# Expert weights of a two-layer backbone: units of 512 KB beside transfers of two neighbouring units

## The chip, the core and the metric

The kernel runs on one core of one Trainium2 chip. Its engines are named as in the profile: PE (matrix), DVE (vector), ACT (scalar), POOL (gpsimd) and SP, whose queue issues the loads from the chip's memory (HBM) that this text is about. The metric is the device time of one execution in microseconds (us), as the median of several runs. All data is fp32.

## The reference, cut to what matters

Two layers over 256 latent tokens and 256 context tokens of width 1024. Layer 0 is a neighbourhood attention and a dense SwiGLU, layer 1 a recurrent block and a top-2-of-8 expert SwiGLU. The change touches the weights of the experts:

```python
def moe_ffn(h, w_router, b_router, w1, w3, w2):
    logits = (h @ w_router).astype(jnp.float32) + b_router.astype(jnp.float32)
    top_v, top_i = lax.top_k(logits, TOP_K)          # TOP_K = 2
    gates = jax.nn.softmax(top_v, axis=-1)
    ...
    for e in range(N_EXPERTS):                       # 8 experts
        y = y + comb[..., e:e + 1] * swiglu(h, w1[e], w3[e], w2[e])
    return y
# swiglu(h, w1, w3, w2) = (silu(h @ w1) * (h @ w3)) @ w2
# w1, w3: 1024 x 3584 and w2: 3584 x 1024 for each expert
```

So the experts' weights are 8 x 3 x 1024 x 3584 x 4 bytes = 352 MB, and all of them are read once.

## The kernel before

**Units.** Every weight is cut on the host into units of 128 partitions x 1024 values (4 KB in each partition, 512 KB in all). Of an expert's weights, a step `s` (seven of them, 512 hidden columns each) has four units of w1, four of w3 and four of w2, so an expert has 84 and all experts 672. The four w2 units of the very last step are laid out differently and come from a tensor of their own, `w2l` (keys "w2c"). In `moe`, the tensor of the other 668, each unit is one contiguous piece of 512 KB.

**Stream.** The class `Stream`, a kind of `Raws`, holds the list of all weight units in the order in which they are used, that of layer 0 and of the recurrent block first. `Raws.load` walks the list: for the next unit it takes the first pool with a free place, allocates a tile called `raw` there and issues the load on SP's queue (L247). A unit is released when it has been used, and its place goes to the next unit in the list. SP works in order: a load that waits for its place holds up all later loads. Each load also waits for one of eight semaphores in turn (DMAHW0 to DMAHW7 in the program's order), so at most eight loads are in flight.

**Places.** The places come from several pools: three of its own (`raw`), and memory that earlier stages leave: eight from the hidden state of the recurrent block (`hp`), four (`rawm`), two (`raw3`), six from the products of the recurrent block (`zp`, three opened first, then a fourth, then all), and for a short time five in tiles that the experts' inputs take later. That makes 23 in the experts' stage.

**Heavy and light experts.** Experts run in a fixed pattern of eight turns. In turns 0, 2, 4 and 6 (heavy; up to 128 tokens) each unit is split by ACT (`whi`, L303) and DVE (`wlo`, L314) into two parts, and PE makes three matmuls of each piece (L1825 to L1827 for w1 and w3, L1758 to L1760 for w2); the unit is released when DVE has made `wlo`. In turns 1, 3, 5 and 7 (light, `LIGHT`; up to 64 tokens) PE reads the raw unit itself (`pair`, L1738), and the unit is released when PE is done. `small_up` does a light step: four rounds of one unit of w1 and one of w3, the units standing in the list in the same order; `w2_step` takes the four w2 units of the step before, and `hidden` turns the step's result. `step` drops in small pieces of the expert before or after (`combine`, `gather`).

```python
            self.nc.sync.dma_start(t, ap() if callable(ap) else ap)      # L247, one unit
                parts.sort(key=lambda x: x[2])                           # light: w1 0, w3 0, w1 1, w3 1, ...
```

Of the kernel before, what the change touches and what calls it, by code (L numbers as in the profile page):

```python
# [117 lines left out]
def lay_out(i):  # L118
# [86 lines left out]
class Rows:  # L205
# [3 lines left out]
    def __getitem__(self, i):  # L209
        _, k, *s = i  # L210
        return self.tiles[k // 2][(slice(None), k % 2, *s)]


class Raws:
    def __init__(self, nc):
        self.nc = nc
        self.pools, self.units, self.raws = [], [], {}
        self.dma_at = self.at = 0

    def add_pool(self, pool, bufs, once=False, n=100, tag="raw", open=None):  # L220
        self.pools.append([pool, bufs if open is None else open, 0, once, bufs, tag])
        self.load(n)
        return self.pools[-1]

    def add_tiles(self, aps, again):
        self.pools.append([None, len(aps), 0, again, aps])
        self.load()

    def widen(self, r, n):
        r[1] = n  # L230
        self.load()

    def add(self, key, ap):
        self.units.append((key, ap))
# [118 lines left out]
def body(tc, nc, es, a, out, upto, dbg):  # L353
# [37 lines left out]
    hh = Rows([hp.tile([P, 2, 512], F32R, name="hh", tag="raw", bufs=8) for _ in range(4)])  # L391
    hl = Rows([hp.tile([P, 2, 512], F32R, name="hl", tag="raw", bufs=8) for _ in range(4)])
# [330 lines left out]
    def moe(p, *i):  # L723
        if p == 0:
            return a["moe"][(0, *i)]
        return lambda: a["moe"][(expert(p), *i)]
# [7 lines left out]
    def add_moe(key, ap):  # L734
        if key[1] in LIGHT:
            st.plain.add(key)
        st.add(key, ap)

    for p in range(NE):
        for s in range(NST):  # L740
            parts = [(nm_, z, i) for nm_, z in (("w1", 0), ("w3", 4)) for i in range(4)]
            if p in LIGHT:
                parts.sort(key=lambda x: x[2])
            for nm_, z, i in parts:
                add_moe((nm_, p, s, i), moe(p, s, z + i))
            if p or s:
                pe, q = divmod(p * NST + s - 1, NST)
                for i in range(4):
                    add_moe(("w2", pe, q, i), moe(pe, q, 8 + i))
    for c in range(4):  # L750
        add_moe(("w2c", NE - 1, c), lambda c=c: a["w2l"][expert(NE - 1), c])
# [17 lines left out]
    sm.add_pool(rawm, RM)  # L769
# [537 lines left out]

    def x_tile(t):
# [11 lines left out]
        xs_ = rawm.tile([P, 2, 512], F32R, name="xcs", tag="raw")  # L1320
        xh, xl_ = xs_[:, 0], xs_[:, 1]
# [38 lines left out]
    def post(q, ri):  # L1360
# [27 lines left out]
        def gated(o):  # L1388
            i, x = divmod(3 * q + o, 2)
            if x == 0:  # L1390
                zq[i] = zp.tile([P, 2, 2, NL], F32R, name="z", tag="raw", bufs=6)
            z = z_t[3 * q + o] = zq[i][:, x, 0], zq[i][:, x, 1]
            cut(*z, hf[o])
# [49 lines left out]
    for i, (kind, n) in enumerate(MIX):  # L1443
# [3 lines left out]
        elif kind == "x":  # L1447
# [6 lines left out]
            if n == 11:  # L1454
                st.add_pool(hp, 8)
            run(4, 3)
        elif kind == "a":
            run(100, 3)
            post(n, gates(n))
            if n == 3:  # L1460
                st.add_pool(rawm, RM)
# [3 lines left out]
                st.add_pool(raw3, RB3)  # L1465
        else:
            if n == (2, 0):
# [8 lines left out]
                once = mp.tile([P, 2, UNIT], F32, name="raw", tag="xs", bufs=1)  # L1476
                once = [once[:, i] for i in range(2)]
                once += [mp.tile([P, UNIT], F32, name="raw", tag=f"xe{y}", bufs=2) for y in "hl"]
                st.add_tiles(once, 4 * AG[0])
# [23 lines left out]
            if n == (0, 7):  # L1503
                zr = st.add_pool(zp, 6, open=3)
            if n == (1, 7):
                st.widen(zr, 4)
# [91 lines left out]
    def gather(p, k):  # L1598
        if k == 0:
            xe[p] = [mp.tile([P, KD, P], F32R, name=f"xe{y}", tag=f"xe{y}", bufs=2) for y in "hl"]  # L1600
# [47 lines left out]
    st.widen(zr, 6)  # L1648
# [162 lines left out]
    def step():  # L1811
        if side:
            side.pop(0)()
# [24 lines left out]
    def small_up(e, s):  # L1838
# [3 lines left out]
        for i in range(4):  # L1842
            for part, nm_ in ((0, "w1"), (1, "w3")):
                u = st.need((nm_, e, s, i))
                for kk in range(2):
                    k = 2 * i + kk
                    pair(
                        (acc[part][0:CAP], acc[part][CAP:P]), x[:, k, j],
                        [u[:, kk * 512 + h * NL:kk * 512 + h * NL + NL] for h in range(2)], k == 0, k == 7,
                    )  # L1850
                if i == 3 and part == 0:
                    sil = mp.tile([P, NL], F32, name="msil", tag="msil", bufs=1)
                    nc.scalar.activation(sil, acc[0], AF.Silu)
                if i == 3 and part == 1:
                    nc.vector.tensor_tensor(sil, sil, acc[1], ALU.mult)  # L1855
                st.done((nm_, e, s, i))
            step()
# [39 lines left out]
    def overflow(p):  # L1897
# [28 lines left out]

        def load(s, i):
            t = raw3.tile([P, UNIT], F32, name="raw", tag="raw")
            nc.sync.dma_start(t, a["moe"][expert(p) if p else 0, s, i])
            return t  # L1930
# [65 lines left out]
```

## Time and profile before

| what | us |
|---|---|
| median of 3 runs (1862.69 to 1865.57) | 1863.77 |
| the profiled execution | 1868.32 |
| its span, first to last instruction | 1866.4 |

| engine | busy us | share of the span | instructions |
|---|---|---|---|
| PE | 1779.2 | 95% | 10067 |
| DVE | 1187.4 | 64% | 1751 |
| ACT | 861.2 | 46% | 1263 |
| POOL | 188.0 | 10% | 195 |

The profiled execution took 4.55 us more than the median; 1.9 us of it lie outside its span. The loads on SP's queue moved 488.03 MB in 138464 packets. A busy PE can still be waiting: its matmuls are pipelined, and their ends are modelled. The experts' stage begins at about 908 us, with the first load of `moe`.

### The profile page before, as it was taken

To read this page: it belongs to the slowest core of one execution; us is meant where nothing else is said; L and a number is where in the kernel's file an instruction comes from. 1 tells how busy PE (TensorE), PEld (TensorE's weight loads), DVE (VectorE), ACT (ScalarE), POOL (GpSimd) and SP (SyncE) were. 2 spreads that over 40 slices of the span, in tenths; PEclk is the share of its full clock that TensorE was granted. 3 is DMA by queue.
4 is the path that set the end of the run, shared out by engine and by line. 5 is a ranking of instruction groups with operands and counts; after the bars stand their busy time and mean duration, and the time that the engine had idled before them with its cause. 6 is when DMAs were issued, how large, how long until landed. Compare 5 with 4: busy or idle time off the path is not lost.

```text
span 1866.4 us, 27907 instructions
## 1 busy us (share of the span) xinstructions
PE 1779.2 (95%) x10067; PEld 1345.7 (72%) x10067; DVE 1187.4 (64%) x1751; ACT 861.2 (46%) x1263; POOL 188.0 (10%) x195
## 2 busy tenths in 40 slices
PE   8998999999999999998878999999999999899997
PEld 6886568888788888786767885588645885378743
DVE  4784776877665457799987961398406972088601
ACT  4434655422313236777645761377215761177500
POOL 1001242100000011353630000000000000000000
PEclk9999999999999999999878999999999999999999
DMA  8444611565764223234556889999999999999996
GB/s 312 159 149 136 219 43 46 190 194 172 246 210 160 91 68 125 79 113 140 199 214 241 301 318 410 408 409 408 409 409 409 408 406 408 406 406 407 403 406 264
DMA packets 138755, 490.02 MB, mean 263 GB/s; under 512 B 15344, under 2 KB 20848, under 8 KB 138608
## 3 DMA queue, kind: packets, MB, share of 16 engines
q1 hardware_dynamic: 138464, 488.03, 69.7%
q8 instruction: 81, 1.33, 0.3%
q14 instruction: 66, 0.54, 0.1%
q10 hardware_dynamic: 144, 0.13, 0.0%
HBM read 487.05 MB, written 1.05 MB: 262 GB/s over the span
## 4 chain that ended last, share of the span: by engine, by line
PE 64%; DMA 18%; DVE 11%; ACT 3%; issue 2%; POOL 2%; SPq 0%; DVEq 0%; ACTq 0%; POOLq 0%
DMA raw<-moe_d 17%; PE ph L1738 5%; PE psa L403 4%; PE psa L404 4%; PE psa L405 4%; PE ph L1825 4%; PE ph L1827 4%; PE ph L1826 4%; DVE wlo L314 3%; PE py L1738 2%; PE py L1758 2%; PE pF L403 2%; PE pF L404 2%; PE py L1760 2%; PE py L1759 2%; PE pF L405 2%
## 5 line engine op out<-in xcount | busy, mean ns | idle before, releaser
L314 DVE TENSOR_TENSOR wlo<-raw,whi 128x1024 fp32r<-128x1024 f32 x480 | 576.2, 1236 | 157.3 <-ACT whi L303 154.8
L303 ACT CAST whi<-raw 128x1024 fp32r<-128x1024 f32 x484 | 493.1, 1050 | 204.4 <-PE pF L404 49.8
L1738 PE MATMUL ph<-raw,xs 128*64 128x256 f32 x1792 | 216.6, 385 | 8.5 <-DMA raw<-moe_d 7.9
L1827 PE MATMUL ph<-wlo,xeh 128*128 128x512 f32 x448 | 177.0, 395 | 6.5 <-DVE wlo L314 6.4
L1825 PE MATMUL ph<-whi,xeh 128*128 128x512 f32 x448 | 179.4, 400 | 1.8 <-ACT whi L303 1.8
L1738 PEld LDWEIGHTS ph<-raw,xs 128*64 128x64 f32 x1792 | 119.4, 136 | 85.1 <-DMA raw<-moe_d 27.9
L1826 PE MATMUL ph<-whi,xel 128*128 128x512 f32 x448 | 176.4, 394 | 0.0
L404 PE MATMUL psa<-hl,whi 128*128 128x512 f32 (+1 forms) x384 | 143.4, 374 | 1.1 <-DVE hl L654 1.0
L403 PE MATMUL psa<-hh,whi 128*128 128x512 f32 (+1 forms) x384 | 144.0, 375 | 0.0
L405 PE MATMUL psa<-hh,wlo 128*128 128x512 f32 (+1 forms) x384 | 142.7, 372 | 0.0
L1855 DVE TENSOR_TENSOR msil<-msil,ph 128x256 f32<-128x256 f32 x28 | 11.8, 420 | 165.6 <-PE ph L1738 165.6
L1738 PE MATMUL py<-raw,mgs 128*64 128x512 f32 (+1 forms) x496 | 107.3, 560 | 6.7 <-DMA raw<-moe_d 5.6
L528 DVE SCALAR_TENSOR_TENSOR macc<-raw,c,macc 128x1024 f32<-128x1024 f32 x84 | 105.3, 1280 | 0.6
L1827 PEld LDWEIGHTS ph<-wlo,xeh 128*128 128x128 f32 x448 | 85.2, 190 | 27.1 <-DVE wlo L314 8.6
L1825 PEld LDWEIGHTS ph<-whi,xeh 128*128 128x128 f32 x448 | 85.3, 190 | 18.9 <-ACT whi L303 2.5
L1826 PEld LDWEIGHTS ph<-whi,xel 128*128 128x128 f32 x448 | 85.3, 190 | 16.9
L1758 PE MATMUL py<-whi,mgh 128*128 128x512 f32 x224 | 87.6, 391 | 0.0
L1760 PE MATMUL py<-wlo,mgh 128*128 128x512 f32 x224 | 87.3, 390 | 0.0
L1759 PE MATMUL py<-whi,mgl 128*128 128x512 f32 x224 | 87.2, 389 | 0.0
L404 PEld LDWEIGHTS psa<-hl,whi 128*128 128x128 f32 x384 | 72.3, 188 | 14.5 <-DVE hl L654 2.3
L403 PEld LDWEIGHTS psa<-hh,whi 128*128 128x128 f32 x384 | 72.3, 188 | 14.2 <-issue 2.1
L405 PEld LDWEIGHTS psa<-hh,wlo 128*128 128x128 f32 x384 | 72.3, 188 | 12.7
(351 smaller groups left out, 3230.4 us busy)
## 6 DMA issues: line engine op xcount, KB each, us to landing
raw<-moe_d SPq DMA_DIRECT2D x668, 512.0 KB, 10.1
raw<-f_d SPq DMA_DIRECT2D x66, 512.0 KB, 3.9
raw<-wm_d SPq DMA_DIRECT2D x64, 512.0 KB, 4.4
raw<-wmh_d SPq DMA_DIRECT2D x32, 512.0 KB, 7.4
raw<-qkv_d SPq DMA_DIRECT2D x24, 512.0 KB, 4.4
raw<-win_d SPq DMA_DIRECT2D x24, 512.0 KB, 3.5
raw<-gat_d SPq DMA_DIRECT2D x14, 512.0 KB, 3.6
raw<-wou_d SPq DMA_DIRECT2D x12, 512.0 KB, 7.3
```

Of the source, the lines that this page charges most:

```text
L303: self.nc.scalar.copy(hi, self.raws[i][0])
L314: eng.tensor_tensor(lo, self.take(key), hi.bitcast(F32), ALU.subtract)
L403: nc.tensor.matmul(o, w[0], x[0], start=first, stop=False)
L404: nc.tensor.matmul(o, w[0], x[1], start=False, stop=False)
L405: nc.tensor.matmul(o, w[1], x[0], start=False, stop=last)
L1738: nc.tensor.matmul(o[h], x, w[h], start=first, stop=last, skip_group_check=True)
L1758: nc.tensor.matmul(ys[e][n], x[0], w[0], start=b, stop=False)
L1759: nc.tensor.matmul(ys[e][n], x[1], w[0], start=False, stop=False)
L1760: nc.tensor.matmul(ys[e][n], x[0], w[1], start=False, stop=l)
L1825: nc.tensor.matmul(acc[part], xh[:, k], w[0], start=(k == 0), stop=False)
L1826: nc.tensor.matmul(acc[part], xl_[:, k], w[0], start=False, stop=False)
L1827: nc.tensor.matmul(acc[part], xh[:, k], w[1], start=False, stop=(k == 7))
```

## The change

In `moe`, two neighbouring units (0 and 1, or 2 and 3, of the same weight and step) now lie side by side: in each partition's row the 4 KB of the first are followed by the 4 KB of the second, and a pair is one piece of 1 MB with rows of 8 KB. A single unit of a pair is then read as rows of 4 KB that lie 8 KB apart.

The places of `hp`, `rawm`, `raw3`, `zp` and the short-lived ones become double-sized (`wide`): 4, 2, 1, 3 (one opened first, then two, then all) and 2 instead of 8, 4, 2, 6 and 4. The three of `raw` and the short-lived one in `ysb` stay single. The number of units that the places hold is the same. For that the tiles of the earlier stages in the same memory are allocated twice as big (`hh`, `hl`, `xcs`, `z`, `xe`). `load` takes a wide place and one transfer of 1 MB (L273) where the next unit is the first of a pair and a wide place is free. Otherwise it loads a single unit (L289) into the first place that is free, and where that is a wide one, the unit after it goes into its other half by a transfer of its own. A wide place is free again when both its units are released.

A light step now takes the units in the order w1 0, w1 1, w3 0, w3 1, w1 2, w1 3, w3 2, w3 3. The code for experts with too many tokens (`overflow`), which isn't entered here, loads pairs too.

```diff

+    twos = lambda w: w.reshape(NE, NST, 2, 2, P, UNIT).transpose(0, 1, 2, 4, 3, 5)
...
-    a["moe"] = np.concatenate([w1, w3, w2], 2)
+    a["moe"] = np.concatenate([twos(w1), twos(w3), twos(w2)], 2)
...
+class Home:
+    def __init__(self, pool, bufs, wide, tag, limit, again, aps):
+        self.pool, self.bufs, self.wide, self.tag = pool, bufs, wide, tag
+        self.limit, self.again, self.aps = limit, again, aps
+        self.used, self.part = 0, None
+
+    def free(self):
+        return self.used < self.limit
+
+    def block(self):
+        self.used += 1
+        if self.pool is None:
+            t = self.aps.pop(0)
+        else:
+            sh = [P, 2, UNIT] if self.wide else [P, UNIT]
+            t = self.pool.tile(sh, F32, name="raw", tag=self.tag, bufs=self.bufs)
+        return [t, 0, self]
+
+    def back(self, b):
+        if self.again is None or self.again > 0:
+            self.used -= 1
+            if self.again:
+                self.again -= 1
+            if self.pool is None:
+                self.aps.append(b[0])
...
     def load(self, n=100):
         while self.dma_at < len(self.units) and n:
             n -= 1
-            for r in self.pools:
-                if r[2] < r[1]:
-                    break
+            i = self.dma_at
+            _, ap, both = self.units[i]
+            r = next((r for r in self.homes if r.wide and r.free()), None) if both else None
+            if r:
+                b = r.block()
+                b[1] = 2
+                self.nc.sync.dma_start(b[0], both())
+                self.raws[i], self.raws[i + 1] = (b[0][:, 0], b), (b[0][:, 1], b)
+                self.dma_at += 2
+                continue
+            r = next((r for r in self.homes if r.part or r.free()), None)
+            if r is None:
+                return
+            if r.part:
+                b, t, r.part = r.part, r.part[0][:, 1], None
+                b[1] += 1
             else:
-                return
-            r[2] += 1
-            t = r[0].tile([P, UNIT], F32, name="raw", tag=r[5], bufs=r[4]) if r[0] else r[4].pop(0)
-            ap = self.units[self.dma_at][1]
+                b = r.block()
+                b[1] = 1
+                t = b[0][:, 0] if r.wide else b[0]
+                if r.wide:
+                    r.part = b
             self.nc.sync.dma_start(t, ap() if callable(ap) else ap)
-            self.raws[self.dma_at] = (t, r)
+            self.raws[i] = (t, b)
...
     def release(self, i):
-        t, r = self.raws.pop(i)
-        if r[0] is None and r[3]:
-            r[3] -= 1
-            r[2] -= 1
-            r[4].append(t)
-        elif r[0] is not None and not r[3]:
-            r[2] -= 1
+        b = self.raws.pop(i)[1]
+        b[1] -= 1
+        r = b[2]
+        if b[1] == 0:
+            if r.part is b:
+                r.part = None
+            r.back(b)
...
-    hh = Rows([hp.tile([P, 2, 512], F32R, name="hh", tag="raw", bufs=8) for _ in range(4)])
-    hl = Rows([hp.tile([P, 2, 512], F32R, name="hl", tag="raw", bufs=8) for _ in range(4)])
+    hh = Rows([hp.tile([P, 4, 512], F32R, name="hh", tag="raw", bufs=4) for _ in range(2)])
+    hl = Rows([hp.tile([P, 4, 512], F32R, name="hl", tag="raw", bufs=4) for _ in range(2)])
...
+        j = (z + i) // 2
+        st.add(key, moe(p, q, j, slice(None), i % 2), None if i % 2 else moe(p, q, j))
...
-                parts.sort(key=lambda x: x[2])
+                parts.sort(key=lambda x: x[2] // 2)
...
-                st.add_pool(hp, 8)
+                st.add_pool(hp, 4, wide=True)
...
-                st.add_pool(rawm, RM)
+                st.add_pool(rawm, RM // 2, wide=True)
...
-                st.add_pool(raw3, RB3)
+                st.add_pool(raw3, RB3 // 2, wide=True)
...
-                zr = st.add_pool(zp, 6, open=3)
+                zr = st.add_pool(zp, 3, wide=True, open=1)
...
+        for part, i in [(part, 2 * ii + j) for ii in range(2) for part in range(2) for j in range(2)]:
+            nm_ = ("w1", "w3")[part]
+            u = st.need((nm_, e, s, i))
+            for kk in range(2):
+                k = 2 * i + kk
+                pair(
+                    (acc[part][0:CAP], acc[part][CAP:P]), x[:, k, j],
+                    [u[:, kk * 512 + h * NL:kk * 512 + h * NL + NL] for h in range(2)], k == 0, k == 7,
+                )
+            if i == 3 and part == 0:
+                sil = mp.tile([P, NL], F32, name="msil", tag="msil", bufs=1)
+                nc.scalar.activation(sil, acc[0], AF.Silu)
+            if i == 3 and part == 1:
+                nc.vector.tensor_tensor(sil, sil, acc[1], ALU.mult)
+            st.done((nm_, e, s, i))
+            if i % 2:
+                step()
```

How SP's order moves. First the loads of the experts' weights whose expert is known beforehand (turn 0), before and after; `wou_d` is the weight before them, `128x2048` a pair, and `order` the table from which the later experts' numbers are read. Before:

```order
L247 DMA raw<-wou_d 128x1024 x12
L247 DMA raw<-moe_d 128x1024 x80
L731 TENSOR_LOAD order
L731 ISA x2
L247 ISA
L247 DMA raw<-moe_d 128x1024
```

After:

```order
L289 DMA raw<-wou_d 128x1024 x12
L289 DMA raw<-moe_d 128x1024 x4
L273 DMA raw<-moe_d 128x2048
L289 DMA raw<-moe_d 128x1024 x14
L273 DMA raw<-moe_d 128x2048 x3
L289 DMA raw<-moe_d 128x1024 x22
L273 DMA raw<-moe_d 128x2048 x3
L289 DMA raw<-moe_d 128x1024 x22
L273 DMA raw<-moe_d 128x2048 x2
L771 TENSOR_LOAD order
```

Of these 80 units 18 come in pairs. Over all 672 units SP issues 140 loads of two units and 392 of one (four of them from `w2l`), 532 instead of 672; the later experts' loads alternate between runs of both kinds in the same way. Eight of the pairs follow directly on the 80 units, so 17 of the 140 are among the first 108 units.

Next the start of SP's loads of `moe`, with the semaphores that each waits for; the numbers in the tiles' names tell places apart. Before:

```order
L247 DMA raw_8188<-moe_d 128x1024 [waits DMAHW3_49,DVE_49]
L247 DMA raw_8241<-moe_d 128x1024 [waits DMAHW4_49,DVE_49]
L247 DMA raw_8288<-moe_d 128x1024 [waits DMAHW5_49,DVE_49]
L247 DMA raw_8293<-moe_d 128x1024 [waits DMAHW6_49]
L247 DMA raw_8295<-moe_d 128x1024 [waits DMAHW7_49,PE_49]
```

After:

```order
L289 DMA raw_8131<-moe_d 128x1024 [waits DMAHW3_49,DVE_49]
L289 DMA raw_8228<-moe_d 128x1024 [waits DMAHW4_49,DVE_49]
L289 DMA raw_8228<-moe_d 128x1024 [waits DMAHW5_49]
L289 DMA raw_8234<-moe_d 128x1024 [waits DMAHW6_49,PE_49]
L273 DMA raw_8236<-moe_d 128x2048 [waits DMAHW7_49,PE_49]
L289 DMA raw_8234<-moe_d 128x1024 [waits DMAHW0_49]
L289 DMA raw_8243<-moe_d 128x1024 [waits DMAHW1_49,DVE_49]
```

The second unit takes a wide place (8228) and so does the third; the second now waits until both units that lay there are released, the third for nothing more. The eight semaphores in turn are as before.

Last PE's order in the first step of a light expert (`ph` are its two sums, `xs` its tokens). Before:

```order
L1804 MATMUL pgt_10118<-con_64,msil_10031 128x128 x4
L1738 MATMUL ph_10127<-raw_9754,xs_9696 64x256 x4
L1738 MATMUL ph_10128<-raw_9776,xs_9696 64x256 x4
L1738 MATMUL ph_10127<-raw_9788,xs_9696 64x256 x4
L1738 MATMUL ph_10128<-raw_9811,xs_9696 64x256 x4
L1738 MATMUL ph_10127<-raw_9823,xs_9696 64x256 x4
L1738 MATMUL ph_10128<-raw_9841,xs_9696 64x256 x4
L1738 MATMUL ph_10127<-raw_9855,xs_9696 64x256 x4
L1738 MATMUL ph_10128<-raw_9873,xs_9696 64x256 x4
```

After:

```order
L1850 MATMUL pgt_10000<-con_64,msil_9915 128x128 x4
L1784 MATMUL ph_10009<-raw_9664,xs_9598 64x256 x8
L1784 MATMUL ph_10010<-raw_9707,xs_9598 64x256 x8
L1784 MATMUL ph_10009<-raw_9735,xs_9598 64x256 x8
L1784 MATMUL ph_10010<-raw_9765,xs_9598 64x256 x8
L1804 MATMUL py0_9157<-whi_10037,mgh_10005 128x512
```

The same 32 matmuls stand there, two units of one sum at a time. The instructions of PE, DVE, ACT and POOL are the same in number and, but for the light steps, in sequence.

## Rows read from the trace of the kernel before

**Rows 1.** The page: DMA traffic in 40 slices of the span, GB/s.

```profile
GB/s 312 159 149 136 219 43 46 190 194 172 246 210 160 91 68 125 79 113 140 199 214 241 301 318 410 408 409 408 409 409 409 408 406 408 406 406 407 403 406 264
```

**Rows 2.** Busy time by stretch; the last two columns are DMA share and GB/s.

```profile
core 0: us, PE busy (x) PEld busy (x) DVE busy (x) ACT busy (x) POOL busy (x), PEclk, DMA share, GB/s
1060.00:1120.00 60.00, 59.06 (x313) 47.62 (x312) 44.11 (x44) 38.23 (x47) 0.00 (x0) 1.00 0.78 282
1120.00:1230.00 110.00, 110.00 (x702) 67.25 (x701) 40.54 (x60) 36.02 (x54) 0.00 (x0) 1.00 1.03 409
1230.00:1430.00 200.00, 194.41 (x1102) 130.45 (x1100) 103.16 (x115) 87.13 (x112) 0.00 (x0) 1.00 1.03 409
...
1750.00:1845.00 95.00, 88.87 (x607) 45.81 (x605) 13.70 (x24) 11.54 (x23) 0.00 (x0) 1.00 1.02 405
```

**Rows 3.** The page: the chain that ended last, shares of the span by engine.

```profile
PE 64%; DMA 18%; DVE 11%; ACT 3%; issue 2%; POOL 2%; SPq 0%; DVEq 0%; ACTq 0%; POOLq 0%
```

**Rows 4.** The chain of waits in order of time: start us, us, what.

```profile
1233.27 10.10 DMA raw<-moe_d
1243.49 10.12 DMA raw<-moe_d
1253.73 10.12 DMA raw<-moe_d
```

**Rows 5.** SP's waits, 1240 to 1420 us: who ended them, us, times, longest.

```profile
SPq L247 <- DMA raw<-moe_d: 102.3, 137, 1.4
SPq L247 <- DVE wlo L314: 3.2, 11, 0.4
```

**Rows 6.** SP's waits, 1000 to 1060 us.

```profile
SPq L247 <- DVE wlo L314: 44.7, 38, 8.3
```

**Rows 7.** DMA packets, 1240 to 1420 us; queue: packets, MB, share of 16 engines.

```profile
DMA packets 20161, 73.54 MB, mean 409 GB/s; under 512 B 2239, under 2 KB 2239, under 8 KB 20147
q1 hardware_dynamic: 20147, 73.36, 102.2%
```

**Rows 8.** DMA packets that start in the 0.1 us from 990.70 us.

```profile
DMA packets 14, 0.06 MB, mean 573 GB/s; under 512 B 0, under 2 KB 0, under 8 KB 14
q1 hardware_dynamic: 14, 0.06, 139.1%
```

**Rows 9.** DMA packets that start in the 0.1 us from 578.30 us.

```profile
DMA packets 7, 0.03 MB, mean 287 GB/s; under 512 B 1, under 2 KB 1, under 8 KB 6
q1 hardware_dynamic: 6, 0.02, 50.2%
q14 instruction: 1, 0.01, 19.3%
```

**Rows 10.** The page: all packets of queue 14.

```profile
q14 instruction: 66, 0.54, 0.1%
```

**Rows 11.** DMA issues from 900 to 1114 us: count, KB each, us to landing.

```profile
raw<-moe_d SPq DMA_DIRECT2D x108, 512.0 KB, 5.4
```

**Rows 12.** The page: all issues of the experts' weights.

```profile
raw<-moe_d SPq DMA_DIRECT2D x668, 512.0 KB, 10.1
```

**Rows 13.** DMA packets, 2.6 to 8.1 us.

```profile
DMA packets 444, 1.61 MB, mean 293 GB/s; under 512 B 45, under 2 KB 54, under 8 KB 444
q1 hardware_dynamic: 444, 1.61, 92.3%
```

**Rows 14.** DMA packets, 8.2 to 10.8 us.

```profile
DMA packets 381, 1.05 MB, mean 406 GB/s; under 512 B 45, under 2 KB 171, under 8 KB 381
q1 hardware_dynamic: 381, 1.05, 101.2%
```

**Rows 15.** PE in order of time near the end; in brackets the idle time before.

```profile
1842.59 1.08 PE L1738 MATMUL ph<-raw,xs 128*64 128x256 f32 x8 [0.20 <-DMA raw<-moe_d]
1847.67 1.08 PE L1738 MATMUL py<-raw,mgs 128*64 128x512 f32 x4 [0.17 <-DMA raw<-moe_d]
1849.63 1.09 PE L1738 MATMUL py<-raw,mgs 128*64 128x128 f32 x16 [0.52 <-ACT mgs L1801]
```

More of the change, by code (lines that the diff above doesn't have):

```diff
@@ L210, in __getitem__ @@
         _, k, *s = i
-        return self.tiles[k // 2][(slice(None), k % 2, *s)]
+        return self.tiles[k // 4][(slice(None), k % 4, *s)]
+class Home:
[20 more added lines that the diff above has]
+                self.aps.append(b[0])
 class Raws:
@@ L216, in __init__, with add_pool, add_tiles, add @@
         self.nc = nc
-        self.pools, self.units, self.raws = [], [], {}
+        self.homes, self.units, self.raws = [], [], {}
         self.dma_at = self.at = 0
-    def add_pool(self, pool, bufs, once=False, n=100, tag="raw", open=None):
-        self.pools.append([pool, bufs if open is None else open, 0, once, bufs, tag])
+    def add_pool(self, pool, bufs, once=False, n=100, wide=False, open=None):
+        self.homes.append(Home(pool, bufs, wide, "raw", bufs if open is None else open, 0 if once else None, None))
         self.load(n)
-        return self.pools[-1]
-    def add_tiles(self, aps, again):
-        self.pools.append([None, len(aps), 0, again, aps])
+        return self.homes[-1]
+    def add_tiles(self, aps, again, wide=False):
+        self.homes.append(Home(None, 0, wide, None, len(aps), again, aps))
         self.load()
     def widen(self, r, n):
-        r[1] = n
+        r.limit = n
         self.load()
-    def add(self, key, ap):
-        self.units.append((key, ap))
+    def add(self, key, ap, both=None):
+        self.units.append((key, ap, both))
     def load(self, n=100):
@@ L723, in moe @@
     def moe(p, *i):
-        if p == 0:
-            return a["moe"][(0, *i)]
-        return lambda: a["moe"][(expert(p), *i)]
+        return lambda: a["moe"][(expert(p) if p else 0, *i)]
     def expert(p):
@@ L732, in expert, with add_moe @@
         return who[p]
-    def add_moe(key, ap):
-        if key[1] in LIGHT:
+    def add_moe(key, z):
+        nm_, p, q, i = key
+        if p in LIGHT:
             st.plain.add(key)
-        st.add(key, ap)
+        j = (z + i) // 2
+        st.add(key, moe(p, q, j, slice(None), i % 2), None if i % 2 else moe(p, q, j))
     for p in range(NE):
@@ L742, in body @@
             if p in LIGHT:
-                parts.sort(key=lambda x: x[2])
+                parts.sort(key=lambda x: x[2] // 2)
             for nm_, z, i in parts:
-                add_moe((nm_, p, s, i), moe(p, s, z + i))
+                add_moe((nm_, p, s, i), z)
             if p or s:
@@ L748, in body @@
                 for i in range(4):
-                    add_moe(("w2", pe, q, i), moe(pe, q, 8 + i))
+                    add_moe(("w2", pe, q, i), 8)
     for c in range(4):
-        add_moe(("w2c", NE - 1, c), lambda c=c: a["w2l"][expert(NE - 1), c])
+        key = ("w2c", NE - 1, c)
+        st.plain.add(key)
+        st.add(key, lambda c=c: a["w2l"][expert(NE - 1), c])
     def dump(name, t):
@@ L768, in body @@
     sm.load()
-    sm.add_pool(rawm, RM)
+    sm.add_pool(rawm, RM // 2, wide=True)
     gq = cp.tile([P, 1], F32, name="gq")
@@ L1306, in g_tile @@
         nc.scalar.activation(ge, p[:, 0:NL], AF.Gelu_apprx_tanh)
+    xs2 = [None]
     def x_tile(t):
@@ L1319, in x_tile @@
             )
-        xs_ = rawm.tile([P, 2, 512], F32R, name="xcs", tag="raw")
-        xh, xl_ = xs_[:, 0], xs_[:, 1]
+        if t % 2 == 0:
+            xs2[0] = rawm.tile([P, 2, 2, 512], F32R, name="xcs", tag="raw", bufs=RM // 2)
+        xh, xl_ = xs2[0][:, t % 2, 0], xs2[0][:, t % 2, 1]
         nc.vector.tensor_copy(xh, xc_)
@@ L1388, in gated @@
         def gated(o):
[L1389 removed]
+            i, x = divmod(3 * q + o, 4)
             if x == 0:
[L1391 removed]
+                zq[i] = zp.tile([P, 4, 2, NL], F32R, name="z", tag="raw", bufs=3)
             z = z_t[3 * q + o] = zq[i][:, x, 0], zq[i][:, x, 1]
@@ L1475, in body @@
                 nm = Norm(tp, 1, 1, lambda: sqs.pop(0))
[L1476 to L1479, printed above, removed]
+                once = [mp.tile([P, 2, UNIT], F32, name="raw", tag=n, bufs=b) for n, b in (("xs", 1), ("xe", 2))]
+                st.add_tiles(once, 2 * AG[0], True)
                 st.add_tiles([mp.tile([P, UNIT], F32, name="raw", tag="ysb", bufs=1)], AG[1])
@@ L1599, in gather @@
         if k == 0:
-            xe[p] = [mp.tile([P, KD, P], F32R, name=f"xe{y}", tag=f"xe{y}", bufs=2) for y in "hl"]
+            t = mp.tile([P, 2, KD, P], F32R, name="xe", tag="xe", bufs=2)
+            xe[p] = t[:, 0], t[:, 1]
         g = (psu if p == 0 and k % 2 else pst)("pg")
@@ L1647, in body @@
     nc.vector.tensor_copy(cnt, pp[:, 0:8])
-    st.widen(zr, 6)
+    st.widen(zr, 3)
     st.hold = False
@@ L1841, in small_up @@
         j = LIGHT.index(e)
[L1842 to L1857, printed above, removed]
+        for part, i in [(part, 2 * ii + j) for ii in range(2) for part in range(2) for j in range(2)]:
[15 more added lines that the diff above has]
+                step()
         return sil
@@ L1925, in overflow @@
         nc.scalar.copy(back, g[:, 0:NL])
+        pair_ = [None]
         def load(s, i):
-            t = raw3.tile([P, UNIT], F32, name="raw", tag="raw")
-            nc.sync.dma_start(t, a["moe"][expert(p) if p else 0, s, i])
-            return t
+            if i % 2 == 0:
+                pair_[0] = raw3.tile([P, 2, UNIT], F32, name="raw", tag="raw", bufs=RB3 // 2)
+                nc.sync.dma_start(pair_[0], a["moe"][expert(p) if p else 0, s, i // 2])
+            return pair_[0][:, i % 2]
         yo = [psu("py0"), psu("py1")]
```

2 lines of the change are left out of this document (1 added, 1 removed).

## The prediction

> **What bounds the kernel now.** I read the GB/s slices of the page first. The reader is to see one figure in them: from the 25th slice on, some 1120 us, the traffic stands at 403 to 410 GB/s in every slice but the last [rows 1]. A rate that no longer depends on what is computed is a limit. The busy times by stretch say the same: the DMA share is 1.02 to 1.03 from 1120 to 1845 us, under heavy and light experts alike, and 0.78 before [rows 2]. PE, at 95% of the span, looks like the bound and is not one there: near the end it stops 0.2 us before each unit for its landing [rows 15], so part of its 1.08 us per unit is waiting inside busy spans. The chain gives PE 64% and DMA 18% [rows 3], since it can be followed through PE as long as PE keeps pace; where it runs through DMA, its pieces are loads of 10.1 us, each starting 10.2 us after the one before [rows 4]. That is eight loads in flight, the number of semaphores that SP takes in turn: 10.2 / 8 = 1.28 us for each unit. SP's own waits agree: between 1240 and 1420 us it waits 102.3 us for landings and 3.2 us for places [rows 5].
>
> Before 1114 us it is otherwise. In turn 0 SP waits for places that DVE releases (44.7 of 60 us, [rows 6]), and DMA has pauses. By 1114 us SP has issued 108 units [rows 11]; the queue is full from there on, and 668 - 108 = 560 units of this tensor [rows 12] and the four of `w2l` follow.
>
> **What one unit costs the queue.** With the packet view over a tenth of a microsecond a single packet's time can be read. In 0.1 us from 990.70 us, 14 packets start, all between 2 and 8 KB (rows of 4 KB); they hold 139.1% of 16 engines x 0.1 us, 2.226 us, so 159 ns each [rows 8]. In 0.1 us from 578.30 us, SP's queue has five such rows and one packet under 512 B, 50.2% or 803 ns; less 5 x 159 this leaves 8 to 9 ns for the small one, the signal of landing, of which each load has one for each of 16 engines [rows 9]. A unit gives every engine eight rows and a signal: 8 x 159 + 9 = 1281 ns. That is the 1.28 us of the chain, so the engines are busy without a hole, and a row's time is the price. Over 180 us it holds too: 20147 packets, 2239 of them small, take 102.2% of 2880 us; that is 163 ns for a row, with some overlap, at 409 GB/s [rows 7].
>
> The window at 578.30 us also holds what the kernel before never asks of SP's queue: one packet of 8 KB, of queue 14, which fetches instructions (66 packets and 0.54 MB on the page, 8.2 KB each [rows 10]). It took 19.3% of 1.6 us, 309 ns, where two of 4 KB take 318 [rows 9]. So about 9 ns of each packet don't depend on its length, as the bare signal says as well.
>
> **The change part by part.**
> *Pairs.* A load of two units has eight rows of 8 KB and one signal for each engine: 8 x 309 + 9 = 2481 ns, against 2 x 1281 = 2562. It saves 81 ns. SP's order has 140 pairs, 17 of them among the first 108 units, where the queue isn't full: their saving becomes pause. 123 pairs remain, 123 x 0.081 = 10.0 us. Bounds: if rows of 8 KB went as two packets, a pair would save its one signal, 9 ns, 1.1 us in all. At the other end stands the 309 ns row. I take 309, since it is the same packet size on the same engines beside the same stream.
> *Single units, now rows of 4 KB at 8 KB pitch.* 560 - 246 = 314 of them come after unit 108. The trace has loads of this very form: the first ones, of the tokens (a row of 8 KB each, read in halves). From 2.6 to 8.1 us some 390 rows took 92.3% of 88 us, about 205 ns each [rows 13]; from 8.2 to 10.8 us, rows of the last such load and 126 shorter ones fill 101.2% of 41.6 us, which leaves about 160 ns for each of 210 rows [rows 14]. The slow ones are the first of the execution, the fast ones stand in a full queue, as these do. I take 0; the other end is 8 x 46 = 0.37 us for each load, 115 us.
> *Places.* 23 units as before, but half of the loads into wide places wait for one release more. Where SP waits for places (turn 0 and the start of turn 1) this delays a load by the 1.1 to 1.4 us between releases, and the next one by nothing. At the moment the queue fills, it costs between 0 and 1.3 us, once. I take 0, since the two halves are then issued together and the queue is never empty after that. Later SP waits for landings, and a place that comes free 1.3 us late is still early [rows 5].
> *Fewer loads.* 140 issues less on SP. SP waits most of its time there [rows 5]: 0.
> *Larger tiles in the earlier stages.* The memory and the readers are the same; SP's loads of `moe` start a unit later at two or three places. Turn 0 takes what lies there 20 us and more after it lands; 0.
> *Order of a light step.* The same 32 matmuls for 8 units, in pairs. PE waits for landings in the last light steps [rows 15], and 12 units take 15.4 us of queue; 0 to -1 us.
> *The tail.* The last w2 units and the four of `w2l` stay single, so what follows the last landing (matmuls from 1849.63 us on, [rows 15]) is moved, not changed.
>
> The sum: 1868.32 - 10.0 = 1858.3 us for the profiled execution. That one took 4.55 us more than the median of the runs, 1863.77 us, so for a median 1863.77 - 10.0 = 1853.8 us. Does PE allow it? It is 100% busy by the records from 1120 to 1230 us [rows 2], because it works off the backlog of turn 0; from 1230 us on the records leave it 5.6 us idle in 200 and 6.1 us in the 95 before 1845 us. Between two heavy turns the queue gains 10.0 / 3.4 = 3 us, and these idle times and the waits inside busy spans cover it.
>
> **Rivals.**
> *Rows are cut.* SP's queue may move no packet over 4 KB; the trace shows none there, only on the queues that fetch instructions. Then a pair saves 9 ns, and the time is 1863.77 - 1.1 = 1862.7 us. For it: no row of SP's queue speaks against it. Against it: the engines take 8 KB packets in the same stretch [rows 9]. The Trainium skill bears on this: the page DMA: Bandwidth & Descriptors, section SWDGE vs HWDGE vs iDMA, gives "≤4096 B preferably" for a packet, where POOL's software makes the descriptors. By that rule the sum would be this rival's; no run here shows how SP's hardware path cuts a row of 8 KB.
> *The memory sets the rate, not the packets.* Then rows of 8 KB change nothing either, and the time is the same 1863 us. Against it: a row takes 159 ns alone and 163 in the full queue [rows 7, 8]. The same page of the Trainium skill, section Bandwidth, says that about 358 GB/s of the memory's side bind for a core's loads; by it no packet size could help here. The trace disagrees, at 409 GB/s [rows 7].
> *Slower: the half rows.* Reading every second 4 KB keeps part of the memory from working, as it may have done for the tokens. The price is 314 loads x 8 rows x the excess of a row, 2.5 us for each nanosecond; from 4 ns on it takes the whole gain. At a fifth of the 46 ns, 9 ns, it costs 23 us: 1863.77 - 10.0 + 23 = 1877 us. For it: [rows 13]. Against it: [rows 14], with the same pitch.
> *The places tie up.* Pairs of units are held until both are used, so SP waits for places again in the light turns, each time with eight loads ahead. It would show as pauses of the queue. At 1.3 us in two places for each pair of experts, 8 x 1.3 = 10 us: 1864 us. Against it: 3.2 us of such waits in 180 us [rows 5].
>
> **Chances and range.** My forecast 0.69, its own range 1851 to 1857 us (10.0 us, less or more the 1.3 us of the start and the spread of the runs, 1.4 us each way). Cut rows or memory 0.16; half rows 0.11; places 0.04, half of it still faster. A difference under 0.2%, 3.7 us, can't be told from no change by a measurement of this kernel. Faster by more: 0.69 + 0.02 = 0.71; within: 0.16 + 0.02 = 0.18; slower: 0.11. For 8 in 10 the range takes the forecast's own and the two cases without effect: 1850 to 1865 us.
>
> **What would show it.** In the profile after: SP's queue has 140 x 128 x 2 packets of 4 KB less and 140 x 128 of 8 KB more, and the count under 8 KB falls by 140 x 272; if rows are cut, the count stays near 138464. The rate from 1120 us on should be (560 + 4) x 0.524 MB over 564 x 1.281 - 10.0 = 712 us, 415 instead of 409 GB/s, and higher where pairs follow each other: 1.049 MB / 2.481 us = 423 GB/s. Rows of 4 KB at 163 ns or less in the full queue clear the half rows; at 167 they have taken all. The DMA share must stay at 1.0 from 1120 to 1835 us; pauses there, with SP waiting for DVE or PE, are the places. I am wrong if the rate in stretches of pairs is 409 GB/s, or if the chain after 1233 us goes through PE.

## The result and the profile after

The changed kernel takes 1857.41 us (median of 17 runs, 1850.36 to 1865.28) against 1866.95 us for the kernel before (17 runs, 1862.00 to 1872.82). The ratio is 0.9944, with a 95% interval of 0.9931 to 0.9957: 10.5 us less, 8.0 to 12.9 by the interval. The forecast was 10.0 us less, a ratio of 0.9947 to the median it started from. (The medians alone differ by 9.5 us.) The time of 1857.41 us lies inside the forecast's range of 1850 to 1865, and 3.6 us above its 1853.8: the median of three runs that it started from, 1863.77, was itself 3.2 us below that of the 17. In the two profiled executions the span went from 1866.35 to 1855.54 us, 10.8 us.

The first view is again the traffic in 40 slices, and under it the counts of the page's DMA part: all packets, then SP's queue (packets, MB, share of 16 engines).

```profile
GB/s 304 162 158 137 217 46 46 164 219 156 232 210 185 96 79 117 80 111 85 214 253 212 325 300 406 412 412 414 416 414 412 412 414 410 413 410 412 414 414 270
DMA packets 118588, 489.96 MB, mean 264 GB/s; under 512 B 13104, under 2 KB 18608, under 8 KB 100528
...
q1 hardware_dynamic: 118304, 488.02, 69.1%
```

The plateau of [rows 1] stands some 5 GB/s higher, with the same bytes. The count under 8 KB fell from 138608 to 100528, by 38080 = 140 x 272, and SP's queue has 20160 = 140 x 144 packets less: each of the 140 pairs went as 128 rows of 8 KB and 16 signals. No row was cut.

The busy times by stretch of the changed kernel (columns as in [rows 2]):

```profile
1060.00:1120.00 60.00, 59.06 (x313) 47.76 (x312) 43.00 (x44) 36.77 (x46) 0.00 (x0) 1.00 0.79 287
1120.00:1230.00 110.00, 109.04 (x694) 65.30 (x693) 40.27 (x60) 35.20 (x54) 0.00 (x0) 1.00 1.02 414
1230.00:1430.00 200.00, 195.31 (x1115) 133.90 (x1114) 106.99 (x119) 90.95 (x117) 0.00 (x0) 1.00 1.02 413
...
1750.00:1835.00 85.00, 78.88 (x562) 42.92 (x559) 11.78 (x22) 10.03 (x21) 0.00 (x0) 1.00 1.02 411
```

The DMA share stays at 1.02 to 1835 us, so no pauses came, and the rate is 411 to 414 GB/s (forecast 415) where it was 405 to 409. Before 1120 us the share is 0.79 where it was 0.78: as forecast, the pairs of turn 0 bring nothing there.

Where ten pairs follow each other, from 1139 to 1158 us, the packets of the changed kernel are:

```profile
DMA packets 1093, 8.00 MB, mean 421 GB/s; under 512 B 118, under 2 KB 118, under 8 KB 118
...
q1 hardware_dynamic: 1092, 7.98, 101.0%
```

Apart from 118 signals all packets have 8 KB. 101.0% of 16 x 19 us are 307.0 us; less 118 x 9 ns, 974 rows took 314 ns each. The forecast had 309 ns and 423 GB/s. Over the 180 us of [rows 7], with pairs and single units mixed:

```profile
DMA packets 15957, 74.49 MB, mean 414 GB/s; under 512 B 1771, under 2 KB 1771, under 8 KB 11975
...
q1 hardware_dynamic: 15943, 74.31, 101.7%
```

In the same 180 us SP waited for (columns as in [rows 5]; L273 issues pairs, L289 single units):

```profile
SPq L289 <- DMA raw<-moe_d: 82.2, 75, 2.1
SPq L273 <- DMA raw<-moe_d: 24.8, 25, 2.0
SPq L273 <- PE ph L1784: 7.1, 5, 4.3
SPq L273 <- DVE msil L1901: 2.2, 1, 2.2
```

With the shorter ones that are not shown, waits for places rose from some 6 to some 16 us and cost nothing that can be seen: the DMA share keeps at 1.02, since a load issued 4 us late still stands behind several others.

The landing times follow the unit's number. Unit 108 lands 0.35 us earlier than before, unit 300 3.2 us, unit 516 8.0 us, the last one 11.08 us (1841.56 instead of 1852.63). So 10.7 us come out of the full queue, spread over its whole length.

### The profile page after: what moved, and what is told of

It is laid out like the page before. It is cut to its first block, busy times and chain, and to the rows that moved or that the text cites. A ratio compares the mean times of both kernels' runs of the same rounds, so it can differ in the third digit from the quotient of the medians.

```text
span 1855.5 us, 27189 instructions
## 1 busy us (share of the span) xinstructions
PE 1771.2 (95%) x10067; PEld 1351.2 (73%) x10067; DVE 1185.9 (64%) x1751; ACT 860.5 (46%) x1263; POOL 188.4 (10%) x195
## 2 busy tenths in 40 slices
DMA packets 118588, 489.96 MB, mean 264 GB/s; under 512 B 13104, under 2 KB 18608, under 8 KB 100528
## 4 chain that ended last, share of the span: by engine, by line
PE 71%; DMA 13%; DVE 10%; ACT 3%; issue 1%; POOL 1%; SPq 0%; DVEq 0%; ACTq 0%; POOLq 0%
DMA raw<-moe_d 12%; PE ph L1784 6%; PE ph L1873 5%; PE ph L1871 5%; PE ph L1872 5%; PE psa L445 4%; PE psa L446 4%; PE psa L447 4%; PE py L1804 3%; PE py L1806 3%; PE py L1805 3%; PE py L1784 3%; DVE wlo L356 2%; PE pF L445 2%; PE pF L446 2%; PE pF L447 2%
## 5 line engine op out<-in xcount | busy, mean ns | idle before, releaser
L1784 PE MATMUL ph<-raw,xs 128*64 128x256 f32 x1792 | 210.2, 383 | 9.1 <-DMA raw<-moe_d 8.8
L1873 PE MATMUL ph<-wlo,xe 128*128 128x512 f32 x448 | 177.3, 396 | 6.9 <-DVE wlo L356 6.8
L1871 PE MATMUL ph<-whi,xe 128*128 128x512 f32 x448 | 179.4, 400 | 2.2 <-ACT whi L345 2.2
L1872 PE MATMUL ph<-whi,xe 128*128 128x512 f32 x448 | 176.2, 393 | 0.0
L1873 PEld LDWEIGHTS ph<-wlo,xe 128*128 128x128 f32 x448 | 85.2, 190 | 28.7 <-DVE wlo L356 10.3
L1871 PEld LDWEIGHTS ph<-whi,xe 128*128 128x128 f32 x448 | 85.0, 190 | 19.2 <-ACT whi L345 2.9
L1872 PEld LDWEIGHTS ph<-whi,xe 128*128 128x128 f32 x448 | 85.3, 190 | 17.0
L447 PEld LDWEIGHTS psa<-hh,wlo 128*128 128x128 f32 x384 | 72.9, 190 | 12.5
## 6 DMA issues: line engine op xcount, KB each, us to landing
raw<-moe_d SPq DMA_DIRECT2D x388, 512.0 KB, 10.8
```

The costliest lines, as they stand in the source:

```text
L447: nc.tensor.matmul(o, w[1], x[0], start=False, stop=last)
L1784: nc.tensor.matmul(o[h], x, w[h], start=first, stop=last, skip_group_check=True)
L1871: nc.tensor.matmul(acc[part], xh[:, k], w[0], start=(k == 0), stop=False)
L1872: nc.tensor.matmul(acc[part], xl_[:, k], w[0], start=False, stop=False)
L1873: nc.tensor.matmul(acc[part], xh[:, k], w[1], start=False, stop=(k == 7))
```

## The experiments

All ratios are to the kernel before, measured beside it on the same chip, with 95% intervals; the kernel before had a median of 1868.25 us beside the first four kernels and of 1868.12 beside the last three. Distances of landings are those in each trace between 1125 and 1820 us; in the kernel before their median is 1.280 us, in the changed one 1.280 for a single unit and 2.491 for a pair.

**All units one by one.** The new layout, the double places and the new order of a light step stay; only the pairs go:

```diff
-        st.add(key, moe(p, q, j, slice(None), i % 2), None if i % 2 else moe(p, q, j))
+        st.add(key, moe(p, q, j, slice(None), i % 2), None)
```

> The changed kernel (new layout, double places, new order of a light step) with every pair issued as two loads of one unit: 672 loads, all of 4 KB rows, most of them half rows at 8 KB pitch. Theory (the gain is the pairs' 8 KB rows, and half rows, places and order cost nothing): ratio to the kernel before 1.000, within 0.002, landings 1.28 us apart in the full queue and a 4 KB row at 163 ns on the mean. Rival 1 (half rows cost something that the pairs paid for): a row of 168 ns or more and 1.01 or above. Rival 2 (the gain came from the places or from the order of the light steps): 0.994 to 0.996 as in the changed kernel.

Measured: 0.9998 (0.9984 to 1.0011). From 1240 to 1420 us its packets are:

```profile
DMA packets 20166, 73.56 MB, mean 409 GB/s; under 512 B 2238, under 2 KB 2238, under 8 KB 20152
...
q1 hardware_dynamic: 20152, 73.38, 102.2%
```

That is [rows 7] but for a few packets; (2943.4 - 2238 x 0.009) / 17914 rows is 163 ns in both. Rows of 4 KB at 8 KB pitch cost nothing, and layout, places and order together move nothing that can be measured (the interval leaves up to 3 us). The gain is the pairs'.

**Pairs of 4 KB rows.** The old layout, and the same 140 loads of two units, out of two places in memory:

```diff
-    a["moe"] = np.concatenate([twos(w1), twos(w3), twos(w2)], 2)
+    a["moe"] = np.concatenate([w1, w3, w2], 2)
...
+    def two(p, q, j):
+        return lambda: a["moe"][(expert(p) if p else 0, q, slice(2 * j, 2 * j + 2))].rearrange("u p n -> p u n")
```

> The changed kernel with the old layout: the same 140 loads of two units in the same order, but each of them as rows of 4 KB, for the two units stand apart in memory. Theory (length of the rows): 123 pairs in the full queue save one signal each, 9 ns, 1.1 us, and SP issues 140 loads less, which by the two long landings that are gone from the changed kernel's queue is 1.4 us: 2.5 us, ratio to the kernel before 0.9987, and a pair lands 2.55 us after the one before it. Rival (fewer loads and signals make the gain, not the rows): 0.9944, and a pair lands after 2.49 us.

Measured: 0.9989 (0.9977 to 1.0002), and a pair 2.560 us after the load before it. The stretch of pairs, 1140 to 1158 us:

```profile
DMA packets 1910, 7.37 MB, mean 409 GB/s; under 512 B 115, under 2 KB 115, under 8 KB 1909
...
q1 hardware_dynamic: 1909, 7.35, 102.2%
```

Half the signals of [rows 7] for the same bytes, yet 409 GB/s. Fewer and larger loads aren't the main point; the length of the packet is. What is left, 2 us, is not cleanly apart from zero by the times; the landings give 1.2948 us for a unit against 1.2984 before, 2.0 us for 564 units.

**More pairs.** A pair that finds no double place waits for one, unless two single places are free:

```diff
             r = next((r for r in self.homes if r.part or r.free()), None)
+            if both:
+                if sum(r.limit - r.used for r in self.homes if not r.wide) < 2:
+                    return
+                r = next(r for r in self.homes if not r.wide and r.free())
             if r is None:
                 return
```

> The changed kernel with another rule for places: a pair that finds no double place free waits for one, unless two single places are free. 302 pairs instead of 140, 254 of them (before 123) after the 108th unit. Theory: each of the 131 more saves 69 ns (landings of 2.491 against 2 x 1.280 us), 9.0 us, and 131 loads less on SP save 2.6 us of long landings (0.69 us for each 128 instructions of SP): 11.7 us less than the changed kernel, ratio to the kernel before 0.988. Rival 1 (PE becomes the bound: its records leave it 18.6 us in all from 1230 to 1845 us): half of that or less, 0.991 to 0.9944, with DMA share under 1.0 in the heavy turns. Rival 2 (waiting for double places makes pauses): SP waits for DVE and PE after 1130 us and 0.9944 or above.

Measured: 0.9890 (0.9871 to 0.9910), a median of 1847.95 us. Its busy times by stretch, and SP's waits from 1130 to 1820 us:

```profile
1230.00:1430.00 200.00, 197.05 (x1128) 137.01 (x1127) 109.57 (x122) 93.22 (x119) 0.00 (x0) 1.00 1.01 419
1430.00:1630.00 200.00, 197.32 (x1128) 139.41 (x1127) 112.34 (x128) 94.16 (x119) 0.00 (x0) 1.00 1.01 419
```

```profile
SPq L273 <- DMA raw<-moe_d: 230.0, 144, 3.0
SPq L273 <- DVE wlo L360: 103.7, 62, 3.7
SPq L273 <- PE ph L1788: 92.0, 55, 4.7
```

The last landing is 11.0 us earlier than in the changed kernel, for 9.0 + 2.6 expected. Of rival 2 half came true: SP waits some 240 us for DVE and PE, counting the shorter waits that are not shown. But the DMA share is 1.01, so those waits lie behind loads in flight. Rival 1 failed too: PE's idle time fell to 2.7 and 2.9 us in 200 and the queue still set the pace. 1.4 us of the gain are lost behind the last landing: 15.3 us to the end instead of 14.0, perhaps since the last two units of `w2` now land together, which no run tells apart. This kernel beats both.

**SP's instruction fetch.** In the kernel before, one landing in 32 comes 0.7 us late. The chain of waits shows it: a load in whose flight a late landing falls takes 10.8 us, the others 10.1.

```profile
1264.01 10.82 DMA raw<-moe_d
...
1274.94 10.12 DMA raw<-moe_d
...
1295.42 10.12 DMA raw<-moe_d
...
1305.65 10.81 DMA raw<-moe_d
```

The two of 10.8 us start 41.64 us apart, 32 loads and a late landing. SP runs four instructions for a load (a wait, two of registers, the DMA), so that is 128 of them. A landing at 1268.41 us was the late one, and 1.7 us ahead of it the packets from 1266.6 to 1266.8 us hold one of 8 KB on the queue of instructions:

```profile
q1 hardware_dynamic: 20, 0.07, 92.2%
q14 instruction: 1, 0.01, 9.8%
```

All 14 landings of the kernel before that are more than 0.4 us late between 1125 and 1820 us come 1.4 to 2.2 us after such a packet, one for each 128 instructions of SP; only after the first three of these 17 packets (1143, 1184 and 1225 us) is no landing that late. The trace also has the time of each of a load's 16 signals, one from each DMA engine. At all 14 the last signal alone slips, by 0.66 to 0.72 us; the median of the other 15 is on time to 0.01 us. So it is one engine that falls behind at each fetch, and the load has landed only when that one has its part.

The changed kernel has the same sign every 31 to 35 loads: its SP has fewer waits to run. Three kernels tell the fetch from the number of loads; a fourth asks whether it adds to the pairs. In the changed kernel with constant addresses:

```diff
-        return lambda: a["moe"][(expert(p) if p else 0, *i)]
+        return lambda: a["moe"][(p, *i)]
```

> The changed kernel with the addresses of all the experts' loads as constants: the experts come in the order of their numbers, so the choice of the turn's expert is left out. The same loads, but without the two register instructions of SP ahead of each. In both traces one landing in 128 instructions of SP is some 0.69 us late (17 times in the kernel before, 15 in the changed one), 1.7 us after a packet of 8 KB on the queue that fetches instructions. Theory (SP's instruction fetch costs the full queue 0.69 us each time): about 425 loads with two instructions less are 6.6 fetches less, 4.6 us less than the changed kernel, ratio to the kernel before 0.992, and the late landings stand twice as many loads apart (60 to 75). Rival (the late landings come with the number of loads or packets, and the fetch only coincides): still every 34 loads, and 0.9944.

Measured: 0.9940 (0.9923 to 0.9958). The interval holds the rival's 0.9944 and ends just above the theory's 0.992, so the time speaks for less than the 4.6 us, if it decides anything. The landings were late by 4.1 us in all, against 7.5 in the changed kernel, so 3.4 of the 4.6 us came. And the late ones don't stand 60 to 75 loads apart: the large ones come at 1325, 1506 and 1684 us, with small ones between. Halving the instructions removed the regular lateness and left another, which the theory had not in it (the last section says where that one comes from).

The same edit in the kernel before:

```diff
-        return lambda: a["moe"][(expert(p), *i)]
+        return lambda: a["moe"][(p, *i)]
```

> The kernel before with the addresses of the experts' loads as constants (the experts come in the order of their numbers; the choice of the turn's expert is left out): 672 loads of 4 KB rows as before, two SP instructions for each instead of four. Theory (each 128 instructions of SP cost the one DMA engine that fetches them some 0.6 us more work than the others, and a load lands when the last engine has its part): 8.75 fetches less in the full queue, at 9.7 us of lateness in 17 fetches 5.0 us less than before, ratio 0.9973; late landings every 64 loads; and the end of the queue, where one engine alone works for 5 us in the kernel before, is shared more evenly. Rival (the lateness hangs on the number of loads, 32 of them): 1.000, and the same end.

Measured: 0.9983 (0.9968 to 0.9998); late by 4.6 us in all against 9.8, so 5.2 us went, at no change of loads or packets. Seven landings more than 0.4 us late are left of the 14, again in a rhythm of their own (1325, 1509 and 1691 us among them), and none of them comes within 3 us after a fetch of SP's, though eight such packets are still there.

Four instructions more for each load, in the changed kernel:

```diff
+            for n in range(4 if p else 0):
+                nc.sync.runtime_assert(e)
```

> The changed kernel with four instructions of SP more ahead of each load of turns 1 to 7, which test that the expert's number isn't zero: nothing else moves, and SP, which waits for landings most of its time, has room for them. Theory (SP's instruction fetches): about 408 loads x 4 / 128 = 12.75 fetches more in the full queue, at 0.69 us each 8.8 us more than the changed kernel, ratio to the kernel before 0.999; a late landing every 16 to 17 loads; and one DMA engine works alone for the last 8 us or more of the queue. Rival (fetches cost the queue nothing): 0.9944, a late landing every 34 loads.

Measured: 1.0001 (0.9985 to 1.0017). The whole gain of the pairs is gone again; the landings are late by 17.8 us, with a large one every 13 to 19 loads for the most part. This settles it against the number of loads. Nor is it SP's own time: from 1240 to 1420 us SP still waits 87 us for landings (107 in the changed kernel).

```profile
SPq L289 <- DMA raw<-moe_d: 65.5, 70, 2.6
SPq L273 <- DMA raw<-moe_d: 21.7, 29, 1.7
```

The end of the queue shows the one engine once more. The DMA share (the last but one column) in the last three steps before the last landing, first in the kernel before, then with constant addresses in it, then with the four more instructions:

```profile
1846.00:1848.00 2.00, 1.63 (x8) 0.40 (x8) 0.00 (x0) 0.00 (x0) 0.00 (x0) 1.00 0.39 156
1848.00:1850.00 2.00, 1.48 (x12) 0.57 (x10) 0.00 (x0) 0.37 (x1) 0.00 (x0) 1.00 0.09 35
1850.00:1852.60 2.60, 2.13 (x26) 1.45 (x24) 0.83 (x3) 0.37 (x1) 0.00 (x0) 1.00 0.09 30
```

```profile
1842.00:1844.00 2.00, 1.68 (x8) 0.39 (x8) 0.00 (x0) 0.00 (x0) 0.00 (x0) 1.00 0.71 287
1844.00:1846.00 2.00, 1.48 (x18) 0.84 (x16) 0.00 (x0) 0.37 (x1) 0.00 (x0) 1.00 0.67 270
1846.00:1848.30 2.30, 1.83 (x22) 1.15 (x18) 0.81 (x3) 0.37 (x1) 0.00 (x0) 1.00 0.35 135
```

```profile
1846.00:1848.00 2.00, 2.00 (x12) 0.66 (x8) 0.00 (x0) 0.00 (x0) 0.00 (x0) 1.00 0.17 68
1848.00:1850.00 2.00, 1.48 (x18) 0.82 (x16) 0.00 (x0) 0.37 (x1) 0.00 (x0) 1.00 0.06 25
1850.00:1852.20 2.20, 1.73 (x20) 1.04 (x18) 0.68 (x2) 0.37 (x1) 0.00 (x0) 1.00 0.08 28
```

A share of 0.06 to 0.09 is one engine of 16, give or take a half. In the first and third kernel one engine works on alone for the last 4 us, with rows that the others had long finished; with fewer instructions ten or so work on until 1846 us. By the signals, the last load's last part comes 3.6 us after the 15 others in the kernel before and 4.7 us with four more instructions, but 0.4 us with constant addresses. Every load lands when the last engine has its part, so this one sets the rate of all.

Both together, the rule of the 302 pairs and, on it, the constant addresses:

```diff
-        return lambda: a["moe"][(expert(p) if p else 0, *i)]
+        return lambda: a["moe"][(p, *i)]
```

> The kernel with 302 pairs, and the addresses as constants (the choice of the turn's expert is left out): are the two effects independent? In the kernel with 302 pairs the landings after 1125 us are late by 4.4 us in all, in the changed kernel with constant addresses by 4.2 us, and in both of them the engines end within 2.5 us of each other. Theory (the fetching engine is no longer the last one, so nothing is left to gain from SP's instructions): ratio to the kernel before 0.988 to 0.990, as with 302 pairs alone. Rival (each fetch still costs 0.69 us): about 254 x 2 / 128 = 4 fetches less, 2.7 us, 0.9875 or below.

Measured: 0.9884 (0.9863 to 0.9905), against 0.9890 for the pairs alone. The interval doesn't shut out the rival's 0.9875; the landings do, at 1.2535 us a unit on the mean against 1.2531 for the pairs alone: nothing more is gained. Between 1125 and 1820 us the seven kernels and the two of the case line up:

| kernel | SP instructions / 128 | landings late in all, us |
|---|---|---|
| pairs and constant addresses | 4.5 | 5.6 |
| changed, constant addresses | 5.8 | 4.1 |
| before, constant addresses | 8.3 | 4.6 |
| 302 pairs | 9.5 | 4.5 |
| pairs of 4 KB rows | 12.4 | 7.9 |
| changed | 12.5 | 7.5 |
| all units one by one | 15.1 | 8.1 |
| before | 16.8 | 9.8 |
| changed, four instructions more | 25.4 | 17.8 |

(Late in all: the sum of the distances of landings, less their number by the kernel's own median for their size. A median that is off by 3 ns moves a sum by about 1 us: with the medians of the 302 pairs the first row would be 4.7.) From 12 fetches up it is 0.54 to 0.70 us for each; below 10 it stays at 4.1 to 5.6 us, whatever SP does.

## Why the prediction was right

*What bounds the kernel.* Right. All but 0.35 us of the gain at the last landing came out of the full queue, and the 302 pairs took another 11 us out of it with PE idle for 1.4% of the time.

*Pairs.* Right in kind, the size 17% too high. By the landings a pair saves 2 x 1.280 - 2.491 = 69 ns, not 81: the row of 8 KB costs 314 ns in the full queue by the packets and 310 by the landing (2.491 less a signal, by eight), not 309. 123 x 0.069 = 8.5 us instead of 10.0. One packet of another queue was a price good to 2%; the saving, a small difference of two such prices, was off by a sixth.

*Fewer loads.* The term that failed: it was put at 0, for SP waits most of its time. SP's time indeed costs nothing, but its instructions have to be fetched, by the DMA engines that carry the weights. The lateness fell from 9.8 to 7.5 us (2.3), and the pairs of 4 KB rows, which have nothing else but fewer signals, measure 2.0 us by landings. 8.5 + 2.3 = 10.8 us; the landings give 10.7 and the span 10.8. Both terms come from the same landings, so that they add up is no check of them; the 2.0 us of the other kernel is one. That the forecast's 10.0 came so near is in part luck: a term too large by 1.5 us and one of 2.3 us that it lacked nearly cancel.

*Single units, places, larger tiles, order of a light step.* All costed at 0, or next to it, and measured in one: 0.9998. The half rows, the rival on the slower side, took 163 ns in the kernel that loads all units one by one, as whole rows did [rows 7]. Of the two bounds taken for them, the rows of a full queue [rows 14] were the ones that held; what slowed those of the first microseconds [rows 13] stays open; it was not the pitch alone.

*Cut rows, and the memory's rate.* Both out, by 20160 packets less and by 421 GB/s in stretches of pairs. The 4096 bytes that the Trainium skill prefers for a packet (the page DMA: Bandwidth & Descriptors, section SWDGE vs HWDGE vs iDMA, quoted in the prediction) are no limit of SP's queue here. The Trainium skill's page DMA: Bandwidth & Descriptors, section Bandwidth, gives 435 GB/s as the ceiling of the fabric beside the 358 of the memory's side; the 421 GB/s here pass the second and stay below the first.

*Places tie up.* Out: SP's waits for places rose to nearly three times as much, and in the kernel with 302 pairs they grew to some 240 us, without a pause of the queue.

*A sign that misled.* The prediction said that it would be wrong if the chain after 1233 us went through PE. It does, for the most part: PE has 71% of the chain of the changed kernel, DMA 13%, where [rows 3] had 64% and 18%. The line of the page, then pieces of the chain in order of time:

```profile
PE 71%; DMA 13%; DVE 10%; ACT 3%; issue 1%; POOL 1%; SPq 0%; DVEq 0%; ACTq 0%; POOLq 0%
```

```profile
1316.41 7.06 PE ph L1784 x64
...
1372.94 18.55 DMA raw<-moe_d
...
1391.51 13.85 DMA raw<-moe_d
```

Yet the next 11 us of queue time came off as well. The chain follows one path, and where PE nearly keeps step with the queue it may take either; the share of DMA, 1.02 throughout, was the better sign.

## What to carry to other kernels

Where loads alone fill the DMA engines, price a packet as a fixed part and a part by its length (here 9 ns and some 37.5 ns for each KB, from 159 ns for 4 KB and 309 for 8 KB), and lay out memory so that rows are longer (8 KB is the longest tried here); a bigger load of the same rows brings next to nothing. Count the instructions of the engine that issues, even when it waits most of the time, since their fetch runs over the same DMA engines: here the landings of 695 us were late by 7.5 to 17.8 us from twelve fetches up, and by some 5 us whatever their number below ten. And let a load wait for the place in which it is cheap: with up to eight loads in flight that wait was free here.

## What the runs showed of the hardware

SP's instructions come in packets of 8 KB on queue 14, one for each 128 instructions. In the nine kernels that queue has 14 to 37 packets between 1125 and 1820 us, and always 9 to 12 more than SP's instructions divided by 128, so the others are not SP's. Where there are 12 or more of SP's, each delays the full queue by 0.54 to 0.70 us on the mean, though the packet itself takes 0.31 to 0.33 us. In the kernel before that is 9.8 us of 1866. The profile doesn't name engines, but the 16 signals of each load show that one engine carries the delay: from 1266 to 1821 us the others' lead over it grows from 0.2 to some 4 us. Why a fetch costs that engine twice its packet stays open.

With fewer than ten fetches another lateness is left, 4.1 to 5.6 us, in steps some 26 and 155 us apart in four kernels (late landings at 1299, 1325, 1482 and 1509 us in one). The traces show where it comes from. Between 1125 and 1820 us some 31 packets of 16 KB on queue 8, also instructions, take 1.07 us each, one for about 256 matmuls and weight loads of PE. In the kernel before with constant addresses, one load soon after each of these 30 packets has its 16 signals late by 1.1 to 1.7 us in sum; seven times the last signal is among them, and those are its seven late landings. All 22 landings more than 0.4 us late in the four kernels come 2.2 to 4.2 us after such a packet. By these numbers a fetch shows in the landings when it falls to the engine that is last, and is hidden when another one is. No run changes PE's fetches, so their price is read from the traces alone.
